# Hybrid decoder trunk on one core: delta rule scaled from both sides, norms from transposed rows, first loads reordered

## The chip, the cores and the metric

The kernel runs on one core of a Trainium2 chip. The metric is the device time of one execution in microseconds; the kernel before takes 1268.85 us, the median of three runs (1268.23 to 1269.07).

## The reference, cut to what matters

Two layers, each a half-step feed-forward block (SwiGLU), a mixing block with three head groups (gated delta rule, windowed attention, spatial gating), cross attention into 256 memory tokens, and a second feed-forward block; then a final norm. All in float32, 256 positions by 1024 channels. The change touches the delta rule of the mixing block and the loads.

```python
def l2_normalize(x):
    return x * lax.rsqrt(jnp.sum(x * x, axis=-1, keepdims=True) + NORM_EPS)

q = l2_normalize(q.reshape(B, S, DN_HEADS, DN_HEAD_DIM)) * (DN_HEAD_DIM ** -0.5)
k = l2_normalize(k.reshape(B, S, DN_HEADS, DN_HEAD_DIM))
...
    kb = k * beta[..., None]
    lower = jnp.where(tri_strict, jnp.einsum('bhncd,bhnsd->bhncs', kb, k) * decay, 0.0)
    eye = jnp.eye(C, dtype=q.dtype)
    t_inv = lax.linalg.triangular_solve(eye + lower, ..., lower=True, unit_diagonal=True)
    u = jnp.einsum('bhncs,bhnse->bhnce', t_inv, v * beta[..., None])
    w = jnp.einsum('bhncs,bhnsd->bhncd', t_inv, kb * jnp.exp(gc)[..., None])
```

## The kernel before, in words

Activations stand transposed, channels on the 128 partitions and the 256 positions in the free dimension. Every large product is made of float32 operands split in two: ACT casts a weight chunk to a high part (tiles wr to wh), DVE subtracts it for the low part (wl), and PE multiplies the parts as fp32r matmuls into banks pg. A product of a 512-column operand (both parts of the activations side by side) and one of 256 columns stand for one 128x128 weight block (`mm2`), or three of 256 columns (`mm3`). Weight chunks are 512 KB; SyncE's queue (SP) loads them in order into four buffers wr.

`Plan` records all operations, then `schedule` (lines 192 to 361) orders them: it simulates the engines with a table of costs, takes on each engine the ready operation of the highest rank (the longest way to the end plus a boost), and on PE subtracts `HOLD` from the rank of an operation whose kind (fp32r or plain fp32) is not that of the last one. `emit` writes the instructions out in this order, so all of them carry line 378. DMAs on SP keep the order in which the program names them.

The start (`trunk`, line 494 on): ACT's queue loads x in four pieces of two channel blocks each (tiles one, from xT), SP's queue loads the gains (sm) and the first four weight chunks. Twelve plain matmuls on zeros keep PE at work until data is there. The first two columns of the feed-forward block run as four banks at once over those four chunks (`two` in `ffn`): 64 matmuls, 16 for each chunk, with a fifth and sixth bank following.

The feed-forward block's second half goes through 11 pairs of chunks of `w_down` (one `wchunk` of 1 MB for 16 weight blocks). Ahead of the first of them `between` is called: in layer 0 it issues the loads of the attention tables (cb, 1248 KB), sm of layer 1 and the last gain, and in both layers those of the memory tokens (`mem_load`, four times 256 KB).

The delta rule (`mixing`, line 864 on): `conv` makes k, q and v (tiles q, channels on partitions, four heads each). `rnorm` squares them on ACT (256 columns) and sums over the channels with plain matmuls against ones, for each head and each half t of the positions (tiles t into ps). beta times the norm's factor (bk) is spread over rows by matmuls against the identity (pb), and the decay mask E is multiplied with it before the product of k with itself. The triangular matrix is inverted in a ladder of levels (blocks of 2 to 64, `LEVELS`), each level two groups of small plain matmuls for both halves t (tiles Mb, tc, uc, Q), with copies on ACT, subtractions and 32x32 transposes on DVE between them. Then come v, k transposed by PE (vb, kt), and the chain of the two chunks: u0, s1, r1, v1, o0, o1 (each a group of four matmuls into one bank ps, moved out by ACT or DVE). While ladder and chain wait for ACT and DVE, PE runs the projections of the other head groups and of the memory keys.

Of the kernel before, what the change touches and what calls it, by code (L numbers as in the profile page):

```python
# [11 lines left out]
F32R = mybir.dt.float32r  # L12
# [5 lines left out]
P = 128  # L18
D = 1024
T = 256  # L20
# [116 lines left out]
class Plan:  # L137
# [9 lines left out]
    BEGIN, RAMP, SLOW, WARM = 0.73, 4.5, 2.6, 7.5  # L147
    KEEP = ("pg", "ps", "wh", "wl", "t")
    HOLD = 2.0
# [42 lines left out]
    def schedule(self, fixed=None):  # L192
# [85 lines left out]
        while left:  # L278
# [43 lines left out]
            if o["method"] == "dma_start":  # L322
                dma_next += e == "DMA"
                feed = max(feed, t + self.FLIGHT) + lat * (self.SLOW if feed < self.RAMP else 1.0)
                lat = feed - t
# [168 lines left out]
def trunk(tc, xT, memT, w, w2, ca_d, cb_d, sm_d, fin_d, lb_d, out):  # L494
# [3 lines left out]
    with ExitStack() as ctx:  # L498
# [25 lines left out]
        hP = [one([2, T]) for i in range(4)]  # L524
        h = [hP[d // 2][:, d % 2, :] for d in range(KD)]
        ca = one([NCA])
# [4 lines left out]
        plan.boost = 1000.0  # L531
        SY.dma_start(sm[0], sm_d[0])
# [166 lines left out]
        class Norm:  # L699
# [4 lines left out]
            def add(self, d, first=False):  # L704
                if self.g is not None:
                    self.x.append(gained(h[d], self.g[:, d:d + 1], xslot(d), first and d % 2 == 0))
# [6 lines left out]
        def ffn(norm, nxt, start=False, between=None):  # L713
# [50 lines left out]
            side = between() if between else None  # L764
            wt = None
# [60 lines left out]
        def mem_load():  # L826
            raw = [S([2, T]) for _ in range(4)]
            for i in range(4):
                SY.dma_start(raw[i], memT[:, 2 * i:2 * i + 2, :])
            return [raw[k // 2][:, k % 2, :] for k in range(KD)]  # L830

        def mem_operands(l):
            m = mem_load()
            if not mem_st:
                mem_st.append(Stats())
                for k in range(KD):
                    mem_st[0].add(m[k])
            return [gained(m[k], sm[l][:, S_XM + k:S_XM + k + 1], S([2, T], F32R))
                    for k in range(KD)]
# [24 lines left out]
        def mixing(l, norm, nxt, xm):  # L864
# [92 lines left out]
            def rnorm(ts, s):  # L957
                v = tiny("qv" + s, [8])
# [8 lines left out]
                for t in range(2):  # L967
                    DVE.tensor_scalar(v[:, 4 * t:4 * t + 4],
                                      pp[t].rearrange("p (a b) -> p a b", a=8)[:, 0:4, 0], EPS, None,
                                      op0=ALU.add)  # L970
                y = tiny("qr" + s, [8])
                rsqrt(y, v, "qn" + s)
                return y

            kT = conv(1, pk0)
            rk = rnorm(kT, "k")
            bk = tiny("bk", [8])
            DVE.tensor_tensor(bk, beta, rk, op=ALU.mult)
            qT = conv(0)
            vT = conv(2)  # L980
# [475 lines left out]
```

## Time and profile before

| what | value |
|---|---|
| median of three runs | 1268.85 us (1268.23 to 1269.07) |
| the profiled execution's own time | 1268.92 us |
| its span, first to last instruction | 1267.1 us |
| mean granted TensorE clock | 0.997 |
| instructions in the span | 22194 |
| DMA, bytes and mean rate | 216.14 MB, 171 GB/s |

Times in the rows are microseconds from the span's start. A group of a timeline or a list of instructions names the engine, the operation, the tile written, the tiles read, the shape and how many instructions it merges. A plain fp32 matmul has two records in the trace, an fp32r matmul and a transpose have one. A matmul's recorded end is modelled; matmuls overlap, so the distance from one start to the next is what one costs in a sequence.

### The profile page before, as it was taken

The numbers are of one execution on the slowest core, as the hardware profiler recorded it, in microseconds if no ns is written. First come the engines' busy times: TensorE is split into PE (matmuls) and PEld (weight loads), VectorE is DVE, ScalarE is ACT, GpSimd is POOL, SyncE is SP. The second block draws the span as 40 slices with busy tenths as digits, with TensorE's granted clock in tenths as the row PEclk, the third lists the DMA queues.
The fourth block names the chain that finished last, engine by engine and source line by source line (L and its number), as shares of the span: only waits on it lengthen the run. The fifth ranks groups of instructions, "written<-read, shape, count | busy, mean of one in ns | idle before, by whom it ended". The sixth has DMA issues, their size and how long they took to land.

```text
span 1267.1 us, 22194 instructions
## 1 busy us (share of the span) xinstructions
PE 1249.3 (99%) x8400; PEld 1128.6 (89%) x8400; DVE 955.6 (75%) x1777; ACT 722.9 (57%) x1289; POOL 26.5 (2%) x69
## 2 busy tenths in 40 slices
PE   8999999999999999999999999999999999999997
PEld 7888889998898988888988888999899989888886
DVE  7776878987875777777677776799978667777764
ACT  6555755835654655555455565576466455655552
POOL 1000000100000000000000000001000000000000
PEclk9999999999999999999999999999999999999998
DMA  6555765433354455556555566554324544555551
GB/s 238 191 192 197 231 213 174 151 117 120 98 182 153 137 179 190 191 170 204 191 178 188 186 203 208 208 171 147 102 100 144 177 146 137 189 190 183 190 192 68
DMA packets 60730, 216.14 MB, mean 171 GB/s; under 512 B 7120, under 2 KB 7504, under 8 KB 60496
## 3 DMA queue, kind: packets, MB, share of 16 engines
q1 hardware_dynamic: 60048, 213.68, 50.8%
q8 instruction: 66, 1.08, 0.4%
q10 hardware_dynamic: 576, 1.05, 0.2%
q14 instruction: 40, 0.33, 0.1%
HBM read 213.65 MB, written 1.05 MB: 169 GB/s over the span
## 4 chain that ended last, share of the span: by engine, by line
PE 76%; issue 15%; DVE 4%; DMA 2%; ACT 2%; ACTq 0%; SPq 0%; POOLq 0%; POOL 0%; DVEq 0%
PE pg L378 69%; PE ps L378 7%; DVE S L378 2%; DVE wl L378 2%; ACT S L378 1%; ACT wh L378 1%; DMA wr<-w 1%; DMA one<-xT 1%; DMA one<-cb 0%; DMA S<-memT 0%; DVE t L378 0%; ACT L378 0%; ACTq L378 0%; DVE xmx L378 0%; ACT t L378 0%
## 5 line engine op out<-in xcount | busy, mean ns | idle before, releaser
L378 ACT CAST wh<-wr 128x1024 fp32r<-128x1024 f32 (+2 forms) x397 | 415.0, 1047 | 434.7 <-issue 245.5
L378 DVE TENSOR_TENSOR wl<-wr,wh 128x1024 fp32r<-128x1024 f32 (+2 forms) x397 | 484.7, 1222 | 229.4 <-ACT wh L378 228.3
L378 PE MATMUL pg<-X,wh 128*128 128x512 f32 (+1 forms) x2224 | 627.6, 353 | 2.1 <-ACT wh L378 2.1
L378 PE MATMUL pg<-X,wl 128*128 128x256 f32 x1808 | 478.5, 281 | 1.1 <-DVE wl L378 0.9
L378 PEld LDWEIGHTS pg<-X,wh 128*128 128x128 f32 x2224 | 378.3, 188 | 49.2 <-ACT wh L378 3.0
L378 PE MATMUL pg<-S,wh 128*128 128x256 f32 (+1 forms) x1560 | 385.2, 327 | 0.7 <-DVE S L378 0.7
L378 PEld LDWEIGHTS pg<-X,wl 128*128 128x128 f32 x1808 | 339.9, 188 | 18.1 <-DVE wl L378 3.7
L378 PE MATMUL pg<-S,wl 128*128 128x256 f32 x1088 | 300.9, 281 | 1.1 <-DVE wl L378 1.1
L378 PEld LDWEIGHTS pg<-S,wh 128*128 128x128 f32 x1560 | 259.3, 188 | 26.3 <-DVE S L378 1.1
L378 PEld LDWEIGHTS pg<-S,wl 128*128 128x128 f32 x1088 | 204.6, 188 | 3.7 <-DVE wl L378 1.4
L378 DVE TENSOR_TENSOR t<-t,pg 128x256 f32<-128x256 f32 x202 | 83.0, 414 | 2.2 <-ACT t L378 2.2
L378 ACT COPY t<-pg 128x256 f32<-128x256 f32 x202 | 73.0, 365 | 12.5 <-PE pg L378 12.5
L378 DVE TENSOR_TENSOR t<-t,t 128x256 f32<-128x256 f32 x157 | 66.0, 422 | 10.7 <-ACT t L378 3.2
L378 PE MATMUL ps<-S,S 128*128 128x256 f32 (+4 forms) x384 | 48.3, 291 | 2.7 <-ACT S L378 1.7
L378 DVE TENSOR_TENSOR t<-t,rbh 128x256 f32<-128x256 f32 x116 | 48.3, 420 | 1.3
L378 PEld LDWEIGHTS ps<-S,S 128*128 128x128 f32 (+2 forms) x384 | 42.0, 178 | 7.4 <-ACT S L378 3.5
L378 PE MATMUL pg<-wh,X 128*128 128x264 f32 (+2 forms) x192 | 45.0, 323 | 0.0
L378 ACT CAST S<-t 128x256 fp32r<-128x256 f32 x88 | 35.8, 407 | 10.2 <-DVE t L378 10.2
L378 ACT ACTIVATE t<-t 128x256 f32<-128x256 f32 x88 | 36.5, 420 | 7.8 <-DVE t L378 7.7
L378 PE MATMUL pg<-wh,S 128*128 128x512 f32 x128 | 40.8, 395 | 0.0
L378 DVE TENSOR_TENSOR S<-t,S 128x256 fp32r<-128x256 f32 x88 | 36.9, 419 | 2.0 <-ACT S L378 1.9
L378 ACT ACTIVATE t<-one 128x256 f32<-128x256 f32 x72 | 29.5, 412 | 8.6 <-DVE one L378 7.7
(184 smaller groups left out, 865.7 us busy)
## 6 DMA issues: line engine op xcount, KB each, us to landing
wr<-w SPq DMA_DIRECT2D x391, 512.0 KB, 3.3
wr<-w SPq DMA_DIRECT2D x4, 528.0 KB, 3.3
S<-memT SPq DMA_DIRECT2D x8, 256.0 KB, 5.9
lb<-lb SPq DMA_DIRECT2D x2, 640.0 KB, 4.6
one<-cb SPq DMA_DIRECT2D x1, 1248.0 KB, 6.1
one<-xT ACTq DMA_DIRECT2D x4, 256.0 KB, 5.5
out<-S SPq DMA_DIRECT2D x3, 256.0 KB, 2.2
wr<-w SPq DMA_DIRECT2D x2, 256.0 KB, 5.3
```

Source lines behind the costliest of these rows:

```text
L378: getattr(self.engines[o["eng"]], o["method"])(*[real(a) for a in o["args"]], **{k: real(a) for k, a in o["kw"].items()})
```

## The change

In the delta rule `rnorm` transposes the four heads of k (and of q) with PE into a bank, and ACT squares each head's 128 columns straight from the bank with a running sum (`accum_out`), which gives the sum of squares with positions on partitions; the eight matmuls against ones go. The transposed first half of k is kept (kt0), so that the later transposition of k goes. The triangular system is scaled on both sides: the spreading of bk over rows (eight matmuls pb) goes, the mask is multiplied with bk of the row, v is multiplied with kn (factor times sum of squares) in place of beta, and u0 and v1 are multiplied with bk as they leave the bank, on DVE in place of an ACT copy. The planner's `HOLD` goes from 2.0 to 3.0, and its costs of early loads change.

The loads: the first piece of x gets the gains of the first norm behind it (x0), ACT's queue loads x0, half of the first weight chunk and the second chunk, SP's queue all else in the order of use, sm last. The memory pieces, and in layer 0 after them the attention tables in four pieces, sm and the last gain, are issued one behind each chunk pair of the second half of the feed-forward block.

```diff
-    BEGIN, RAMP, SLOW, WARM = 0.73, 4.5, 2.6, 7.5
+    BEGIN, RAMP, SLOW, WARM = 0.73, 10.0, 1.33, 7.5
-    HOLD = 2.0
+    HOLD = 3.0
...
-        SY.dma_start(sm[0], sm_d[0])
-        for i in range(4):
-            SA.dma_start(hP[i], xT[i])
-            for c in ((slice(0, 512), slice(512, 1024)) if i == 0 else (slice(0, 1024),)):
-                SY.dma_start(first[i][:, c], w[i][:, c])
+        SA.dma_start(x0, x0_d)
+        SY.dma_start(first[0][:, lo], w[0][:, lo])
+        SA.dma_start(first[0][:, hi], w[0][:, hi])
+        SY.dma_start(hP[1], xT[0])
+        SA.dma_start(first[1][:, 0:1024], w[1])
+        SY.dma_start(hP[2], xT[1])
+        SY.dma_start(first[2][:, 0:1024], w[2])
+        SY.dma_start(hP[3], xT[2])
+        SY.dma_start(first[3][:, 0:1024], w[3])
+        SY.dma_start(sm[0], sm_d[0])
...
         def late_consts():
-            SY.dma_start(cb, cb_d)
-            SY.dma_start(sm[1], sm_d[1])
-            SY.dma_start(fin, fin_d)
+            c = [slice(i * NCB // 4, (i + 1) * NCB // 4) for i in range(4)]
+            return [lambda s=s: SY.dma_start(cb[:, s], cb_d[:, s]) for s in c] + [
+                lambda: SY.dma_start(sm[1], sm_d[1]), lambda: SY.dma_start(fin, fin_d)]
...
                     if i % 16 == 0:
                         wt = wchunk()
+                        if later:
+                            later.pop(0)()
...
-                pp = [sbank([256]) for _ in range(2)]
-                for i in range(NH):
-                    sq = tmp()
-                    act(sq, ts[i], AF.Square)
-                    for t in range(2):
-                        PE.matmul(pp[t][:, 32 * i:32 * i + P], lhsT=sq[:, t * P:t * P + P],
-                                  rhs=ones, start=True, stop=True)
+                for t in range(2):
+                    ps = hmm(lambda o, i: PE.transpose(o, ts[i][:, tsl(t)], ident))
+                    for i in range(NH):
+                        act(tmp(P), ps[:, i, :], AF.Square, accum_out=v[:, 4 * t + i:4 * t + i + 1])
+                    rows.append(ps)
...
+            rk, vk, krows = rnorm(kT, "k")
+            kt0 = S([NH, P])
+            ACT.copy(kt0, krows[0])
...
-                pb = hmm(lambda o, i: PE.matmul(
-                    o, lhsT=bk[:, 4 * t + i:4 * t + i + 1].to_broadcast([P, P]), rhs=ident,
-                    start=True, stop=True))
                 eb = S([NH, P])
-                DVE.tensor_tensor(eb, es, pb, op=ALU.mult)
+                DVE.tensor_tensor(eb, es, bcl(bk[:, 4 * t:4 * t + 4]), op=ALU.mult)
...
-                DVE.tensor_tensor(v, ps, bcl(beta[:, 4 * t:4 * t + 4]), op=ALU.mult)
+                DVE.tensor_tensor(v, ps, bcl(kn[:, 4 * t:4 * t + 4]), op=ALU.mult)
...
-            ps = hmm(lambda o, i: PE.transpose(o, kT[i][:, 0:P], ident))
-            kt = S([NH, P])
-            DVE.tensor_tensor(kt, ps, bcl(kc), op=ALU.mult)
+            kt = kt0
+            DVE.tensor_tensor(kt, kt, bcl(kc), op=ALU.mult)
...
-            ACT.copy(u0, ps)
+            DVE.tensor_tensor(u0, ps, bcl(bk[:, 0:4]), op=ALU.mult)
...
-            ACT.copy(v1, ps)
+            DVE.tensor_tensor(v1, ps, bcl(bk[:, 4:8]), op=ALU.mult)
```

How the order of the instructions moves, at three places. First the start, on SP's queue and on ACT's: before, SP issues the gains, then the weight chunks (wr from w; the first chunk in two halves).

```order
L378 DMA one_6_69<-sm 128x97
L378 DMA wr_83<-w 128x512 x2
L378 DMA wr_100<-w 128x1024
L378 DMA wr_106<-w 128x1024
L378 DMA wr_112<-w 128x1024
L378 DMA one_5_119<-ca 128x256
```

With the change, the same stretch of SP's queue (xT are three of the four pieces of x), and ACT's queue up to its first cast of a weight chunk:

```order
L378 DMA wr_69<-w 128x512
L378 DMA one_2_82<-xT 128x512
L378 DMA one_3_92<-xT 128x512
L378 DMA wr_98<-w 128x1024
L378 DMA one_4_104<-xT 128x512
L378 DMA wr_110<-w 128x1024
L378 DMA one_6_117<-sm 128x97
L378 DMA one_5_126<-ca 128x256
```

```order
L378 DMA one_1_63<-x 128x520
L378 DMA wr_69<-w 128x512
L378 DMA wr_90<-w 128x1024
L378 ACT_TABLE_LOAD
L378 ACTIVATE X_120<-one_1_63 128x256
L378 ACTIVATE t_130<-one_1_63 128x256
L378 ACTIVATE t_132<-one_1_63 128x256
L378 CAST wh_136<-wr_69 128x512 x2
```

Three of the four x pieces moved from ACT's queue to SP's, half of the first weight chunk and all of the second the other way; the gains moved behind all of these.

Second, SP's queue in layer 0 at the second half of the first feed-forward block, before (cb are the attention tables, memT the memory tokens):

```order
L378 DMA wr_1356<-w 128x1024
L378 DMA one_15_1360<-cb 128x2496
L378 DMA one_7_1365<-sm 128x97
L378 DMA one_8_1372<-fin 128x8
L378 DMA S_1378<-memT 128x512
L378 DMA S_1386<-memT 128x512
L378 DMA S_1393<-memT 128x512
L378 DMA S_1399<-memT 128x512
L378 DMA wr_1404<-w 128x1024
```

and with the change, where the pattern goes on with three more memT and then the four pieces of cb:

```order
L378 DMA wr_1365<-w 128x1024
L378 DMA wr_1406<-w 128x1024
L378 DMA S_1413<-memT 128x512
L378 DMA wr_1438<-w 128x1024
L378 DMA wr_1471<-w 128x1024
L378 DMA S_1480<-memT 128x512
```

Seven loads in one block became one load behind every two weight chunks.

Third, PE in the ladder of layer 0, its first two groups of small matmuls and what stands between them (tc and Mb into one bank for each half t, then Q and uc), before:

```order
L378 MATMUL ps_3202<-tc_85,Mb_3130 64x64 x4
L378 MATMUL ps_3209<-tc_89,Mb_3136 64x64 x4
L378 MATMUL pg_3195<-X_1775,wh_3052 128x256 x2
L378 MATMUL pg_3195<-X_1775,wl_3061 128x256
L378 MATMUL pg_3195<-X_1854,wh_3052 128x256 x2
L378 MATMUL pg_3195<-X_1854,wl_3061 128x256
L378 MATMUL pg_3195<-X_1933,wh_3052 128x256
L378 MATMUL ps_3234<-Q_96,uc_3112 64x64 x4
L378 MATMUL ps_3239<-Q_104,uc_3118 64x64 x4
```

and with the change:

```order
L378 MATMUL ps_3315<-tc_84,Mb_3196 64x64 x4
L378 MATMUL ps_3324<-tc_96,Mb_3210 64x64 x4
L378 MATMUL ps_3329<-one_5_126,q_2749 128x128
L378 MATMUL pg_3260<-wh_3262,X_1995 128x512
L378 MATMUL pg_3260<-wl_3273,X_1995 128x512
L378 MATMUL pg_3260<-wh_3262,X_1995 128x512
L378 MATMUL pg_3260<-wh_3262,X_2074 128x512
L378 MATMUL ps_3347<-Q_88,uc_3187 64x64 x4
L378 MATMUL ps_3352<-Q_102,uc_3204 64x64 x4
```

The ladder now starts later in PE's order, beside the projection with 512 columns, and a single transposition of v (ps from q) stands behind each group.

## Rows read from the trace of the kernel before

**Rows 1.** Page, section 1: busy us, share of the span, instructions of PE.

```profile
PE 1249.3 (99%) x8400; PEld 1128.6 (89%) x8400; DVE 955.6 (75%) x1777; ACT 722.9 (57%) x1289; POOL 26.5 (2%) x69
```

**Rows 2.** PE's waits: released by which engine's tile, us in total, times, longest.

```profile
PE ps L378 <- ACT S L378: 1.7, 2, 0.9
...
PE ps L378 <- DVE S L378: 0.9, 2, 0.5
```

**Rows 3.** Groups by form, PE: shapes, count, busy us, mean ns, idle before.

```profile
L378 PE MATMUL ps<-one,q 128*128 128x128 f32 x24 | 4.3, 286 | 0.0
...
L378 PE MATMUL ps<-one,bk 128*128 128x128 f32 x32 | 3.9, 275 | 0.0
```

**Rows 4.** Timeline, PE, mixing of layer 0: start, us, operation [idle before].

```profile
257.18 1.95 PE L378 MATMUL ps<-one,bk 128*128 128x128 f32 x16
258.96 1.06 PE L378 MATMUL ps<-q 128*128 128x128 f32 x8
...
297.25 0.66 PE L378 MATMUL ps<-one,q 128*128 128x128 f32 x4
297.66 0.48 PE L378 MATMUL pg<-S,wh 128*128 128x256 f32 x2
```

**Rows 5.** Timeline, PE, the start.

```profile
1.05 5.49 PE L378 MATMUL ps<-one 128*128 128x128 f32 x24 [1.05 <-DVE one L378]
6.94 0.73 PE L378 MATMUL pg<-X,wh 128*128 128x512 f32 x2 [0.40 <-ACT wh L378]
...
14.21 0.40 PE L378 MATMUL pg<-X,wh 128*128 128x512 f32 x1
14.44 0.28 PE L378 MATMUL pg<-X,wl 128*128 128x256 f32 x1
14.56 0.40 PE L378 MATMUL pg<-X,wh 128*128 128x512 f32 x1
...
21.64 0.39 PE L378 MATMUL ps<-X,wh 128*128 128x512 f32 x1
```

**Rows 6.** Windows: stretch, its us, busy us by engine, clock, DMA share, GB/s.

```profile
0.00:5.00 5.00, 3.95 (x18) 3.95 (x19) 1.00 (x3) 2.36 (x4) 2.95 (x21) 1.00 0.62 188
```

**Rows 7.** DMA queues from 3 to 6 us, q1 SP's, q10 ACT's: packets, MB, share.

```profile
q1 hardware_dynamic: 275, 0.51, 64.2%
q10 hardware_dynamic: 296, 0.53, 47.9%
```

**Rows 8.** Timeline, ACT and DVE, the start.

```profile
11.29 1.03 ACT L378 CAST wh<-wr 128x1024 fp32r<-128x1024 f32 x1
11.30 0.42 DVE L378 TENSOR_TENSOR t<-t,t 128x256 f32<-128x256 f32 x1
11.63 0.48 DVE L378 SCALAR_TENSOR_TENSOR X<-one,one,X 128x256 fp32r<-128x256 f32 x1
...
12.35 1.23 DVE L378 TENSOR_TENSOR wl<-wr,wh 128x1024 fp32r<-128x1024 f32 x1 [0.23 <-ACT wh L378]
```

**Rows 9.** Timeline, SP, PE and ACT, second half of the feed-forward block, both layers.

```profile
120.26 0.43 SPq L378 DMA_DIRECT2D one<-cb  x1
...
132.89 0.39 PE L378 MATMUL pg<-X,wl 128*128 128x256 f32 x1 [0.67 <-DVE wl L378]
...
135.00 1.05 ACT L378 CAST wh<-wr 128x1024 fp32r<-128x1024 f32 x1 [1.32 <-DMA wr<-w]
...
140.02 0.39 PE L378 MATMUL pg<-S,wl 128*128 128x256 f32 x1 [1.13 <-DVE wl L378]
...
756.43 0.39 PE L378 MATMUL pg<-X,wl 128*128 128x256 f32 x1 [0.28 <-DVE wl L378]
```

**Rows 10.** Timeline, PE, two steps of the ladder in layer 0.

```profile
269.56 1.15 PE L378 MATMUL ps<-tc,Mb 128*64 128x64 f32 x16
...
271.65 1.15 PE L378 MATMUL ps<-Q,uc 128*64 128x64 f32 x16
```

**Rows 11.** Windows: the ladder of layer 0 (PE, PEld, DVE, ACT, POOL).

```profile
269.56:309.88 40.32, 40.32 (x363) 35.03 (x362) 34.17 (x88) 20.76 (x44) 1.59 (x8) 1.00 0.36 118
```

More of the change, by code (lines that the diff above doesn't have):

```diff
@@ L323, in schedule @@
                 dma_next += e == "DMA"
-                feed = max(feed, t + self.FLIGHT) + lat * (self.SLOW if feed < self.RAMP else 1.0)
+                feed = max(feed, t + self.FLIGHT + 0.3 * (t < 1.0)) + lat * (self.SLOW if feed < self.RAMP else 1.0)
                 lat = feed - t
@@ L521, in act @@
             ACT.activation(o, i, f, **kw)
-        hP = [one([2, T]) for i in range(4)]
+        x0 = one([2 * T + KD])
+        hP = [x0[:, 0:2 * T].rearrange("p (a b) -> p a b", a=2)] + [one([2, T]) for i in range(3)]
         h = [hP[d // 2][:, d % 2, :] for d in range(KD)]
+        gain0 = x0[:, 2 * T:]
         ca = one([NCA])
@@ L705, in add @@
                 if self.g is not None:
-                    self.x.append(gained(h[d], self.g[:, d:d + 1], xslot(d), first and d % 2 == 0))
+                    self.x.append(gained(h[d], self.g[:, d:d + 1], xslot(d), first and d == 0))
                 else:
@@ L763, in ffn @@
             plan.boost = 0.0
-            side = between() if between else None
-            wt = None
+            wt, side, later = None, None, []
+            if between:
+                side, later = between()
             for d in range(KD):
@@ L824, in trunk, with mem_operands, two @@
         mem_r, mem_st = [], []
[L826 to L833, printed above, removed]
+        def mem_operands(l, xm):
             if not mem_st:
                 mem_st.append(Stats())
[L836 to L839, printed above, removed]
+            def two(i):
+                raw = S([2, T])
+                SY.dma_start(raw, memT[i])
+                for e in range(2):
+                    k = 2 * i + e
+                    if l == 0:
+                        mem_st[0].add(raw[:, e, :], boost=0.0)
+                    xm.append(gained(raw[:, e, :], sm[l][:, S_XM + k:S_XM + k + 1], S([2, T], F32R)))
+            return [lambda i=i: two(i) for i in range(4)]
         def mem_keys(xm):
@@ L955, in conv @@
                 return res
-            def rnorm(ts, s):
-                v = tiny("qv" + s, [8])
-                pp = [sbank([256]) for _ in range(2)]
-                for i in range(NH):
-                    sq = tmp()
-                    act(sq, ts[i], AF.Square)
-                    for t in range(2):
-                        PE.matmul(pp[t][:, 32 * i:32 * i + P], lhsT=sq[:, t * P:t * P + P],
-                                  rhs=ones, start=True, stop=True)
[L967 to L980, printed above, removed]
-            rq = rnorm(qT, "q")
             def tsl(t):
@@ L990, in hmm, with rnorm @@
                 return ps
+            def rnorm(ts, s):
+                v = tiny("qv" + s, [8])
+                rows = []
+                for t in range(2):
[3 more added lines that the diff above has]
+                    rows.append(ps)
+                DVE.tensor_scalar(v, v, EPS, None, op0=ALU.add)
+                y = tiny("qr" + s, [8])
+                rsqrt(y, v, "qn" + s)
+                return y, v, rows
+            kT = conv(1, pk0)
+            rk, vk, krows = rnorm(kT, "k")
+            kt0 = S([NH, P])
+            ACT.copy(kt0, krows[0])
+            bk = tiny("bk", [8])
+            DVE.tensor_tensor(bk, beta, rk, op=ALU.mult)
+            kn = tiny("kn", [8])
+            DVE.tensor_tensor(kn, rk, vk, op=ALU.mult)
+            qT = conv(0)
+            vT = conv(2)
+            rq = rnorm(qT, "q")[0]
             M, A, U, Mc, Uc, Tc, Qc = [], [], [], [], [], [], []
@@ L1110, in mixing @@
             r1 = S([NH, P])
-            DVE.tensor_tensor(r1, ps, bcl(wc), op=ALU.mult)
+            DVE.tensor_tensor(r1, ps, bcl(egs[:, 0:4]), op=ALU.mult)
             DVE.tensor_tensor(r1, vb[1], r1, op=ALU.subtract)
@@ L1312, in cross @@
             proj_add(ops, range(KD), nxt)
-        norm = Norm(sm[0][:, S_F1:S_F1 + 8])
+        norm = Norm(gain0)
         for d in range(KD):
@@ L1321, in side @@
             def side():
-                if l == 0:
-                    late_consts()
-                return mem_operands(l)
+                xm = []
+                return xm, mem_operands(l, xm) + (late_consts() if l == 0 else [])
             xm = ffn(norm, nxt, l == 0, side)
@@ L1348, in _pack @@
     ins = {}
-    ins["xT"] = f["x"][0].reshape(T, KD // 2, 2, P).transpose(1, 3, 2, 0)
-    ins["memT"] = f["mem"][0].reshape(T, KD, P).transpose(2, 1, 0)
+    t = f["x"][0].reshape(T, KD // 2, 2, P).transpose(1, 3, 2, 0)
+    ins["x0"] = np.concatenate([t[0].reshape(P, 2 * T), f["ffn1_norm"][0].reshape(KD, P).T], 1)
+    ins["xT"] = t[1:]
+    ins["memT"] = f["mem"][0].reshape(T, KD // 2, 2, P).transpose(1, 3, 2, 0)
     def cols2(wm, c0, c1):
```

10 lines of the change are left out of this document (6 added, 4 removed).

## The prediction

> **What bounds the kernel now.** I read the page's busy times first, then what PE waited for, then PE's timeline where the change works. PE is busy in 99% of the span [rows 1], so the question for each part is what it takes from PE's sequence or from PE's few waits. The waits that the profile names are small; those for bank contents in the delta rule (on ACT S and DVE S) come to 2.6 us in the whole span [rows 2]. The recorded length of a matmul is no price, since matmuls overlap: the spread of bk has 0.275 us for each record [rows 3], but eight of these matmuls, 16 records, start at 257.18 and the next group at 258.96 [rows 4], which is 0.2225 us for a matmul. The starts are the prices below.
>
> **The change part by part.**
>
> *Norms and scaling of the delta rule.* For each layer 16 plain matmuls against ones (k and q, four heads, two halves) and eight for the spread of bk go: 24 x 0.2225 = 5.34 us. Sixteen transposes for the norms come and four for k go, so 12 more. Four transposes start at 297.25 and the next work at 297.66 [rows 4]: 0.10 us each, 1.23 us for 12. Net 4.1 us for a layer, **8.2 us** for two, all of it on PE's own sequence.
>
> Here a row and a rule stand apart. The transposes' recorded mean is 0.286 us [rows 3], their distance 0.10. The Trainium skill (TensorE: Matmul & The Clock Gate, Part 4: PE-mode transpose) gives about 275 ns for a 128x128 transpose within a kernel, which agrees with the recorded length; taken as the price it would leave 4.1 us of this term. I take the distance, since it is what PE's sequence shows; the other is a rival below.
>
> What moves to other engines: for each norm eight ACT squares of 128 columns with a sum in place of four of 256, for u0 and v1 a DVE product in place of an ACT copy, and an ACT copy for kt0. In the order of the changed program two whole projections (96 matmuls of 256 columns, 96 x 0.12 = 11.5 us) stand between the transposes of k and the first product that needs its norm, so I cost them at nothing; without that cover the squares alone would be some microseconds a layer. In the chain behind the ladder, a DVE product replaces an ACT copy of the same 512 elements twice; PE's waits there could shrink by some of the 2.6 us [rows 2], or grow. I take zero between a gain of 1.3 (half of them) and a loss that the first rival prices.
>
> *Kept together longer (`HOLD`).* I counted how often PE goes over from fp32r to plain fp32 work: 73 times before, 72 with the change. Into groups of 64-column products, the ladder's among them, it goes 24 times in each program. So no term; what it does is to change what stands between the ladder's steps.
>
> *The start.* Warm-up products run to 6.54, the first real one starts at 6.94, and the next bank's work begins at 21.64 [rows 5]. Between lie 64 products over four chunks, 32 of 512 columns at 0.23 (14.21 to 14.44) and 32 of 256 at 0.12 (14.44 to 14.56) [rows 5]: 11.2 us, 2.8 a chunk. So 3.9 us of the stretch is something else: two sums for the norm, which stay (I take 0.4, two plain matmuls), and waits for data, 3.5. That is the upper bound of the gain. For the lower bound, nothing: the same bytes come through the same engines.
>
> My value follows the second chunk, now third on ACT's queue. Both queues got about the same bytes while both had work: 0.51 and 0.53 MB in three microseconds, 0.35 MB/us together [rows 7]. ACT's three loads are 1.05 MB, so with as much from SP's queue 2.1 MB have moved when this chunk is there; 0.94 MB have by 5.0 (188 GB/s) [rows 6], the rest takes 3.3, so 8.3. The cast takes 1.03 (the ACT row at 11.29) [rows 8]: 9.4, and PE, through with the first chunk at 6.54 + 2.8 = 9.34, waits 0.1. The low part takes 1.23 [rows 8], to 10.65, four products of high parts 0.93, so 0.25 more. From then on DVE sets the pace: two operands at 0.48, two additions at 0.42 and one low part at 1.23 [rows 8] make 3.03 for a chunk against PE's 2.8, and in the fourth chunk the low part is wanted with the second product already; carried through, that is 0.3 and 0.5 us. Waits 1.15, and 0.1 for each of four restarts: 1.55 against 3.5, so **2.0 us** less. The gains' load goes to the end of SP's queue, but they come with x0, and sm is first needed long after. What is late next is therefore DVE's low part, not a load.
>
> *The loads inside the feed-forward block.* In layer 0 the attention tables are issued in one piece at 120.26, with the memory tokens behind; ACT then waits 1.32 us at 135.00 for a weight chunk, and PE twice for a low part, 0.67 at 132.89 and 1.13 at 140.02. Layer 1, with the memory tokens alone, has 0.28 at 756.43 [rows 9]. With the change a load of 0.26 to 0.32 MB follows every 1.05 MB of weights; 1.37 MB take 3.9 us at 0.35 MB/us [rows 7], and PE needs 16 x 0.35 = 5.6 for the blocks of such a chunk [rows 5]. So all of these waits should go: **2.1 us**, bounds 0 and 2.1. What comes with the memory pieces (squares, gained parts on ACT and DVE) is the same work, spread over four chunks.
>
> *Sum.* 8.2 + 2.0 + 2.1 = 12.3 us from the profiled execution's 1268.92, which is 0.07 over the median: **1256.6 us**. The end of the kernel is not touched.
>
> **The rivals.**
>
> *The ladder and chain become exposed.* PE's removed work stood beside a chain through ACT and DVE that isn't shorter. If that chain sets the end of the mixing block, PE waits for what it no longer does. At worst all 8.2 us come back: 1264.8. For it: the chain already has most of PE's named waits in this block [rows 2]. Against: in the ladder PE was busy in all of 40.32 us [rows 11], so PE and not the chain set its pace, and its tightest steps, 269.56 to 271.65, 2.09 us [rows 10], held with no idle time. In the changed order the same step has a transpose and four products of 512 columns between its groups, 0.10 + 0.93 us, in place of seven of 256, 0.83; no later step is given less than the tightest of before, but for the last group of the ladder.
>
> *The loads bring nothing.* Start and tables move the same bytes, and the two queues share the engines; were the data as late as before, only the PE term is left: 1260.7. For it: the first 13 us run near the measured rate. Against: the order of need brings the first 0.77 MB together, and the waits at 132.89 and 140.02 stand beside one block of loads.
>
> *A transpose costs its recorded length.* 24 more transposes at 0.286 in place of 0.10 cost 4.4 us: 1261.0. The starts in [rows 4] speak against it. The Trainium skill's 275 ns (same page and section) would come to nearly this.
>
> *Slower: the ladder is late by one big operation at each step.* Two layers, five levels of two steps: 20 steps, each a short ACT copy or DVE subtraction that PE waits for. In order behind a low part (1.23 us [rows 8]) each would come that much later: 24.6 us, so 1256.6 + 24.6 = 1281.2. It decides from about 0.75 us a step, where the 12.3 us are gone and 2.5 more. For it: DVE was busy for 34.17 of the ladder's 40.32 us [rows 11], and u0 and v1 now need it too. Against: the same share left PE no idle time before.
>
> That the change doesn't take the work from PE is ruled out: the built program has 24 matmuls fewer, 48 plain ones out and 24 transposes in.
>
> **How the numbers follow.** Forecast 0.70; the exposed ladder and chain 0.11; loads without effect 0.12; dear transposes 0.04; the late ladder 0.03. A measurement of this kernel can tell some 0.2% (2.5 us) from no change. All cases but the last are faster by more, except where the first rival also meets a start that gains nothing: faster 0.93, same 0.04, slower 0.03. The range goes down to all upper bounds nearly together (8.2 + 3.5 + 2.1 + 1.3 = 15.1, so 1253.8; I write 1253.5) and up past the loads rival and the dear transposes, and through the better part of the first rival: 1262.5.
>
> **What would show it.** Right: PE's plain 128-column products against ones in the delta rule and the spread of bk gone; the first real product right behind the warm-up, and the fifth bank's first product near 19.6 in place of 21.64; no PE wait for a low part near 130 to 140; PE still near 99% busy, the mixing block of a layer about 4 us shorter. Wrong: new PE waits for S, Mb, Q or uc in the ladder or chain (the first or the last rival), waits for wh in the first 20 us (the loads), or groups of four transposes more than 0.15 us apart.

## The result, and the profile after

The changed kernel takes 1255.55 us (1254.98 to 1255.83, four runs), the kernel before 1268.54 on the same chip (1268.01 to 1269.07, four runs): a ratio of 0.9897 (95% interval 0.9881 to 0.9913), 13.0 us less. 12.3 less had been forecast. The profiled execution has a span of 1254.1 us where before it was 1267.1.

PE's busy time fell with the span, DVE's is the same to the tenth (955.6 us), and ACT has 1.4 us more; the rows of before are [rows 1]. The page of the changed kernel, section 1:

```profile
PE 1238.5 (99%) x8328; PEld 1119.5 (89%) x8328; DVE 955.6 (76%) x1774; ACT 724.3 (58%) x1338; POOL 28.2 (2%) x69
```

So PE is still what sets the time; its busy time fell by 10.8 us, the idle time beside it makes the rest. The list of PE's waits after the change (who released it, us in total, times, longest), against [rows 2]:

```profile
PE ps L378 <- DVE S L378: 1.8, 3, 0.7
PE ps L378 <- ACT S L378: 1.6, 2, 0.8
...
PE ps L378 <- DVE rcm L378: 1.3, 1, 1.3
...
PE pg L378 <- DVE wl L378: 0.2, 1, 0.2
```

The same list of before has 2.1 us for high parts (wh) and this for low parts (wl):

```profile
PE pg L378 <- DVE wl L378: 2.1, 3, 1.1
```

So the waits for weight parts are down to 0.2 us, the waits for S on ACT and DVE have grown by 0.8 us in all, and one is new in this list: 1.3 us for rcm, the factor of the memory tokens' norm.

Where the time went is best read from the starts of PE's matmuls, cut at the same product of both programs (in us; the forecast beside it):

| stretch | before | after | change | forecast |
|---|---|---|---|---|
| start, to the fifth bank | 21.87 | 19.51 | -2.36 | -2.0 |
| layer 0, first half of the feed-forward block | 78.23 | 77.81 | -0.42 | 0 |
| its second half, to 165 us | 65.00 | 64.27 | -0.73 | -1.8 |
| on to the mixing block | 34.59 | 34.60 | 0 | 0 |
| mixing, layer 0 | 167.99 | 164.13 | -3.86 | -4.1 |
| cross and second feed-forward block, layer 0 | 270.04 | 269.68 | -0.36 | 0 |
| first feed-forward block, layer 1 | 183.31 | 182.72 | -0.59 | -0.3 |
| mixing, layer 1 | 168.12 | 164.68 | -3.44 | -4.1 |
| from there to the last matmul | 271.43 | 270.46 | -0.97 | 0 |

The three parts of the change show, and besides them 1.75 us in three stretches that it doesn't touch. Of the last one's 0.97 us, 0.26 belong to the execution and not to the program. The granted clock of PE fell near the end, after idle times of 1.43 and 1.61 us. In the profile of before it is 0.50 (the level of 1.2 GHz) from 1259.5 us on, and the last four records start 0.37 and then 0.21 us apart; in that of the changed kernel it is still 1.00 (2.4 GHz) there, and they start 0.21 and then 0.11 apart:

```profile
1259.98 1.22 PE L378 MATMUL ps<-one,rch 128*128 128x128 f32 x4 [1.61 <-DVE rch L378]
```

```profile
1247.53 0.71 PE L378 MATMUL ps<-one,rch 128*128 128x128 f32 x4 [1.61 <-DVE rch L378]
```

The changed kernel's second profile (after_again, below) has the clock at 0.50 there and 1.22 us again. That profile also bounds what a single stretch can tell: its start is 0.33 us longer and its stretch from 97 to 161 us (the third line) 0.35 shorter than in the first.

**The start.** PE's timeline after the change (start, us, operation, idle before), against [rows 5]:

```profile
6.37 0.50 PE L378 MATMUL pg<-X,wh 128*128 128x512 f32 x1
7.10 0.39 PE L378 MATMUL pg<-X,wl 128*128 128x256 f32 x1 [0.23 <-DVE wl L378]
...
9.85 1.19 PE L378 MATMUL pg<-X,wh 128*128 128x512 f32 x4
11.11 0.74 PE L378 MATMUL pg<-X,wl 128*128 128x256 f32 x4
...
13.08 1.09 PE L378 MATMUL pg<-X,wh 128*128 128x512 f32 x4
14.00 0.65 PE L378 MATMUL pg<-X,wl 128*128 128x256 f32 x4
...
15.87 0.40 PE L378 MATMUL pg<-X,wh 128*128 128x512 f32 x1
...
19.28 0.39 PE L378 MATMUL ps<-X,wh 128*128 128x512 f32 x1
```

The first real product stands right behind the warm-up here, but that is chance: in after_again the warm-up ends at 5.40, since its products go from 0.21 to 0.11 us apart sooner, and the first product starts at 6.70, after 1.29 us of waiting for ACT's high part. The chunks begin at 6.37, 9.85, 13.08 and 15.87; the third takes 2.79 us, which is PE's own pace, the first two 3.48 and 3.23, the fourth 3.41 with 0.37 for the norm's sums. The fifth bank's first product is at 21.05 to 21.64 in the three profiles with the old loads and at 18.90 to 19.61 in the ten with the new ones, so the 2.36 us are good to some 0.5; between the means lie 2.1. The second chunk was there for ACT at 8.75 (8.3 had been forecast):

```profile
8.75 1.05 ACT L378 CAST wh<-wr 128x1024 fp32r<-128x1024 f32 x1 [0.48 <-DMA wr<-w]
```

**The mixing block.** PE's timeline of layer 0 after the change; ps<-one,q are transposes (in groups those for the norms, single ones those of v), ps<-one,g and ps<-q plain matmuls, and 64-column products are the ladder's:

```profile
250.78 0.27 PE L378 MATMUL ps<-one,q 128*128 128x128 f32 x1
250.89 1.06 PE L378 MATMUL ps<-one,g 128*128 128x128 f32 x8
251.78 1.06 PE L378 MATMUL ps<-q 128*128 128x128 f32 x8
252.68 0.93 PE L378 MATMUL ps<-one,q 128*128 128x128 f32 x7
253.36 0.36 PE L378 MATMUL pg<-wh,X 128*128 128x256 f32 x1
...
273.37 1.15 PE L378 MATMUL ps<-tc,Mb 128*64 128x64 f32 x16
274.44 0.33 PE L378 MATMUL ps<-one,q 128*128 128x128 f32 x1
274.53 0.47 PE L378 MATMUL pg<-wh,X 128*128 128x512 f32 x1
...
275.62 1.15 PE L378 MATMUL ps<-Q,uc 128*64 128x64 f32 x16
```

Seven transposes start at 252.68 and the next product at 253.36: 0.10 us each. The groups by form (shapes, count, busy us, mean ns, idle before) have the transposes with a recorded mean of 0.293 us, and no group ps<-one,bk any more, against [rows 3]:

```profile
L378 PE MATMUL ps<-one,q 128*128 128x128 f32 x48 | 10.1, 293 | 0.0
```

The ladder's first two steps (273.37, 275.62) are 2.25 us apart, 2.09 in [rows 10], with no idle time ahead of them, and the window over the ladder, up to the first product of the chain behind it (304.95), has PE busy in every microsecond, as [rows 11] had:

```profile
273.37:305.00 31.63, 31.63 (x313) 27.80 (x312) 28.87 (x80) 15.42 (x37) 1.59 (x8) 1.00 0.33 104
```

Outside of this window PE waits more than before: 0.65 us at 314.67 (0.47 at 319.98 before), and in layer 1 one wait is new, ahead of the product of k with itself:

```profile
871.12 0.94 PE L378 MATMUL ps<-q,q 128*128 128x128 f32 x6 [0.53 <-DVE S L378]
```

**The loads.** The waits at 132.89, 140.02 and 756.43 [rows 9] are gone. In their place the timeline of all engines has this, from DVE's low part to the product that spreads rcm over the partitions:

```profile
148.62 1.22 DVE L378 TENSOR_TENSOR wl<-wr,wh 128x1024 fp32r<-128x1024 f32 x1
...
149.75 0.15 DVE L378 TENSOR_SCALAR rv<-ps 128x2 f32<-128x2 f32 x1
...
149.98 0.70 POOL L378 TENSOR_TENSOR rcm<-rv,one 128x2 f32<-128x2 f32 x1 [130.95 <-DVE rv L378]
...
151.32 0.16 DVE L378 SCALAR_TENSOR_TENSOR rcm<-rna,rcm 128x2 f32<-128x2 f32 x1
...
151.53 0.71 PE L378 MATMUL ps<-one,rcm 128*128 128x128 f32 x4 [1.31 <-DVE rcm L378]
```

Five short operations on DVE and POOL, one behind the other, with a low part ahead of the first: the factor leaves DVE 0.05 us before PE's product starts. In the kernel before the spreading product started 3.6 us after its factor was done. By the trace, what makes the factor late begins at ACT, which waits for the last memory piece:

```profile
144.19 0.73 ACT L378 ACTIVATE t<-S 128x256 f32<-128x256 f32 x2 [2.15 <-DMA S<-memT]
```

Behind these squares stands the cast of a weight chunk (145.62), behind that DVE's low part (146.68), the one at 148.62 and then the factor's first operation at 149.75; in in_one, where ACT doesn't wait for memory tokens at this place, it is at 148.34.

### The profile page after: what moved, and what is told of

The parts are those of the page before. It is cut to its first block, busy times and chain, and to the rows that moved or that the text cites. A ratio compares the mean times of both kernels' runs of the same rounds, so it can differ in the third digit from the quotient of the medians.

```text
span 1254.1 us, 22081 instructions
## 1 busy us (share of the span) xinstructions
PE 1238.5 (99%) x8328; PEld 1119.5 (89%) x8328; DVE 955.6 (76%) x1774; ACT 724.3 (58%) x1338; POOL 28.2 (2%) x69
## 3 DMA queue, kind: packets, MB, share of 16 engines
q10 hardware_dynamic: 432, 1.05, 0.2%
HBM read 213.66 MB, written 1.05 MB: 171 GB/s over the span
## 4 chain that ended last, share of the span: by engine, by line
PE 79%; issue 15%; DVE 3%; ACT 1%; DMA 1%; POOL 0%; ACTq 0%; POOLq 0%; DVEq 0%
PE pg L378 72%; PE ps L378 7%; DVE S L378 2%; DVE wl L378 1%; ACT wh L378 1%; DMA wr<-w 1%; ACT S L378 0%; POOL qrk L378 0%; DVE mx L378 0%; ACT L378 0%; POOL brs L378 0%; DVE xmx L378 0%; ACTq L378 0%; DVE q L378 0%; POOLq L1463 0%
```

## The experiments

All times are medians beside the kernel before on the same chip and in the same rounds: 1267.46 us for the first four, 1268.29 for the next four, 1268.08 for the last four. A ratio stands with its 95% interval.

### dr_only: the delta rule's part alone

The edit to the kernel before: norms from transposes and scaling from both sides, as in the change's hunks in `rnorm` and `mixing`; loads, `HOLD` and the planner's costs stay.

> The kernel before with the delta rule's part of the change alone (norms from transposed rows, scaling from both sides); loads, HOLD and the planner's load costs as before. Theory (the gain is PE's own sequence: 48 plain matmuls out at 0.2225 us, 24 transposes in at 0.10): about 8.2 us less than before, 1260.3 or within 1 us of it. Rival (the ladder and the chain set the end of the mixing block): 4 us less or fewer, with new PE waits for Mb, Q, uc or S. Rival (a transpose costs its recorded 0.286 us): 3.8 us less.

Measured: 1261.94 us (1260.21 to 1262.34), ratio 0.9950 (0.9936 to 0.9963). Both mixing blocks are shorter by what they are in the full change: 3.82 and 3.33 us (3.86 and 3.44). But the total gains only 5.5 us, less than the theory's 7.2 to 9.2. Part of it is given back in layer 1's feed-forward block, which this edit doesn't touch: its second half takes 85.70 us in place of 84.84, with the same order of products, since PE waits 0.9 us for low parts there in place of 0.3 (PE's waits from 730 to 825 us; the first line is of this kernel, the second of the kernel before):

```profile
PE pg L378 <- DVE wl L378: 0.9, 2, 0.6
```

```profile
PE pg L378 <- DVE wl L378: 0.3, 1, 0.3
```

Why isn't shown. That the mixing block ends sooner is not needed for it: in placed (below), whose blocks end as late as before, the wait there is 0.57 us. With the change's loads it is gone.

### loads_only: start and loads alone

The edit to the kernel before: the start's loads, gains with x0, memory tokens (laid out as in the changed kernel) and tables spread over the chunks, and the planner's load costs; the delta rule and `HOLD` stay.

> The kernel before with the loads alone (x0 and the order at the start, memory and tables spread behind weight chunks, the planner's load costs); delta rule and HOLD as before. Theory: 2.0 to 2.4 us at the start and 1 to 2 us in the feed-forward block, together 3 to 4.1 us less than before. Rival (the same bytes are as late as before): no difference over 0.5 us.

Measured: 1264.22 us (1262.75 to 1265.41), ratio 0.9973 (0.9963 to 0.9984). The start is 2.5 us shorter, but the stretch from 100 to 165 us takes 65.08 against 65.00: nothing gained. The list of PE's waits of this kernel says why:

```profile
PE ps L378 <- DVE t L378: 2.0, 1, 2.0
...
PE pg L378 <- DVE wl L378: 0.2, 1, 0.2
```

The waits for low parts are gone here as well, and 2.0 us go to t, the memory tokens' squares, whose sum PE wants before the last pieces have come and been squared. It is the same norm that makes the 1.3 us for rcm in the full change.

### hold2: the changed kernel with `HOLD` at its old value

```diff
-    HOLD = 3.0
+    HOLD = 2.0
```

> The changed kernel with HOLD back at 2.0. In the built order PE goes over from fp32r to plain fp32 work 75 times in place of 72. Theory of the prediction (no term for HOLD): within 0.5 us of the changed kernel. Rival (each such group costs some 0.3 us around its edges): about 0.9 us slower than the changed kernel.

Measured: 1256.31 us (1256.11 to 1256.49), ratio 0.9908 (0.9895 to 0.9922), span 1254.3 us against 1254.1. `HOLD` is worth nothing that can be told apart from zero; the rival's 0.9 us lie within the interval too, and only the spans, 0.2 us apart, speak against it.

This run shows one thing more. The two parts alone brought 5.5 and 3.2 us; together, in this kernel and in the same rounds, it is 11.2, so 2.4 more than their sum. The profiles show 1.3 of it, 0.8 of this in layer 1's feed-forward block, where dr_only's added wait is gone; the rest isn't placed.

### t_twice: the transposes for the norms issued twice

```diff
                     ps = hmm(lambda o, i: PE.transpose(o, ts[i][:, tsl(t)], ident))
+                    for i in range(NH):
+                        PE.transpose(ps[:, i, :], ts[i][:, tsl(t)], ident)
```

> The changed kernel with the 32 transposes of the two norms (both layers) issued twice into the same banks. Theory (0.10 us for a transpose in a sequence): 3.3 us slower than the changed kernel. Rival (a transpose costs its recorded 0.286 us): 9.2 us slower.

Measured: 1262.55 us (1261.57 to 1264.41), ratio 0.9959 (0.9947 to 0.9972), 6.2 us more than hold2 beside it. The two mixing blocks take 6.3 us more than in the changed kernel, 0.2 for each of 32 transposes: between the two prices. PE's timeline of this kernel shows that it is two things:

```profile
253.16 1.04 PE L378 MATMUL ps<-one,q 128*128 128x128 f32 x8
254.04 1.95 PE L378 MATMUL ps<-q 128*128 128x128 f32 x16
...
277.68 0.68 PE L378 MATMUL ps<-tc,Mb 128*64 128x64 f32 x8
278.29 0.33 PE L378 MATMUL ps<-one,q 128*128 128x128 f32 x1
278.37 0.48 PE L378 MATMUL pg<-wl,X 128*128 128x512 f32 x1
278.78 0.68 PE L378 MATMUL ps<-Q,uc 128*64 128x64 f32 x8
```

Eight transposes in 0.88 us are 0.11 each, so 32 cost 3.5. The rest, 2.8 us, is the planner's answer: it cut steps of the ladder in two (8 records in place of 16), and half a step takes 0.61 us (277.68 to 278.29) where a whole one takes 1.07 (273.37 to 274.44 above), so 0.15 for each of three cuts in a layer. Two more changes from fp32r to plain work in each layer, and in layer 1 a wait of 0.68 us for tc that the changed kernel doesn't have, are in it as well. So the price of a transpose is the distance, 0.11 us. The Trainium skill (TensorE: Matmul & The Clock Gate, Part 4: PE-mode transpose) gives about 275 ns; the recorded length agrees with it (0.293 in the changed kernel), the time that a transpose takes from PE's sequence does not.

### after_again: the changed kernel, unedited

> The changed kernel once more, without an edit, as the mark for the three others on this chip. Expected: the ratio of the first comparison, 0.990 of the kernel before (0.988 to 0.992), some 1255 us; a ratio outside of 0.987 to 0.993 would mean that the chip, not the program, sets a part of the difference.

Measured: 1256.09 us (1255.80 to 1256.48), ratio 0.9904 (0.9891 to 0.9918). It is the mark for the next three.

### m_late: the memory norm's factor without a boost

```diff
-                plan.boost = 60.0
+                plan.boost = 60.0 if tag == "h" else 0.0
```

> The changed kernel, but the factor of the memory tokens' norm is placed without a boost, so its spread over the partitions comes later in PE's order. Theory: the 1.31 us that PE waits at 151.53 for rcm is a matter of order alone (the factor is put into PE's order before VectorE can have it) and goes: the stretch from 100 to 165 us shrinks by 1.1 to 1.4, the whole by about 1.3 us against the changed kernel. Rival: the factor is late because VectorE is, and whatever needs VectorE's next low part waits then instead: less than 0.3 us.

Measured: 1257.75 us (1256.84 to 1257.86), ratio 0.9916 (0.9902 to 0.9929): slower by 1.7 us. Neither theory. The stretch from 100 to 165 us did lose 2.2 us against the mark (61.73 in place of 63.92, in part since four small products left it), but the wait came back in the mixing block, longer:

```profile
240.41 0.68 PE L378 MATMUL ps<-one,rcm 128*128 128x128 f32 x4 [1.61 <-DVE rcm L378]
```

and with these products there the planner gave layer 0 the same cut-up ladder as in the run with doubled transposes: 168.0 us for the block in place of 164.1. In this run too the factor's spread stands in PE's order ahead of when it can be done, though its rank is lower.

### placed: the kernel before, its tiles where the changed kernel has them

```diff
+        for tag in """one1s0 one9s0 one11s0 wrs0 xss0 xss1 ... fnas1""".split():
+            sb.tile([P, 1], F32, tag=tag, name="place_" + tag)
         for o in order:
...
-        hP = [one([2, T]) for i in range(4)]
+        x0 = one([2 * T + KD])
+        hP = [x0[:, 0:2 * T].rearrange("p (a b) -> p a b", a=2)] + [one([2, T]) for i in range(3)]
```

> The kernel before with its order untouched, but every tile in SBUF at the address that it has in the changed kernel (the tiles' tags are named in that kernel's order ahead of the first instruction, and the first input tile is 8 columns wider). Theory: 256-column products start 0.1170 us apart in the changed kernel and 0.1179 before because of where the operands lie; then the feed-forward and cross blocks take the changed kernel's times (the feed-forward block behind the first cross block 0.3 to 0.5 us less, the one of layer 1 0.4 each half, about 1.5 to 2.0 us in all), with nothing gained at the start, in the mixing blocks' groups or in the waits at 130 to 140. Rival: the pace comes from the other order of the loads; then the time is that of the kernel before, within 0.4 us.

Measured: 1268.17 us (1267.49 to 1270.12), ratio 1.0002 (0.9993 to 1.0010): no change. The theory falls as it was put: the addresses of the tiles' slots alone do not bring the shorter untouched blocks (the second feed-forward block of layer 0 takes 186.19 us, 186.02 before, 185.72 after). More on this in the last section.

### in_one: memory tokens and tables in one piece again

```diff
                 side, later = between()
+                while later:
+                    later.pop(0)()
...
-                return xm, mem_operands(l, xm) + (late_consts() if l == 0 else [])
+                return xm, (late_consts() if l == 0 else []) + mem_operands(l, xm)
```

> The changed kernel, but the memory tokens and tables are loaded in one piece where the down projection begins, tables first, as before. Theory: the waits for low parts behind that block of loads (0.67, 1.13 and 0.28 us in the kernel before) come back, and the 1.31 us wait for the memory norm's factor changes with the earlier squares: between 0.5 and 2.1 us longer than the changed kernel. Rival: spreading the loads brings nothing by itself, since what is saved at the low parts is given back at the factor: within 0.4 us of the changed kernel, or shorter.

Measured: 1254.12 us (1253.48 to 1254.34), ratio 0.9887 (0.9872 to 0.9902): 2.0 us under the mark, and the ranges of the two don't touch. The theory was wrong in its sign. The stretch from 100 to 165 us takes 62.93 (63.92 in the mark). Windows over it (us, busy us of PE, PEld, DVE, ACT, POOL, clock, DMA share, GB/s), of the changed kernel first:

```profile
100.00:165.00 65.00, 63.69 (x366) 55.46 (x365) 50.04 (x90) 38.68 (x72) 0.70 (x1) 1.00 0.67 215
```

```profile
100.00:165.00 65.00, 65.00 (x373) 56.50 (x372) 50.18 (x90) 41.21 (x76) 0.70 (x1) 1.00 0.68 220
```

With the loads in one block PE is idle for nothing, 1.31 us with the loads spread. The waits for low parts did not come back, and the one for rcm went. So spreading the loads isn't needed to remove the old waits, and it is what made the new one.

### in_one_again: the same once more

> The version with the memory tokens and tables loaded in one piece, tables first and in four parts, once more as the mark for the next two. Expected: the ratio of its first run, 0.9887 of the kernel before (0.9872 to 0.9902), about 2 us under the changed kernel.

Measured: 1253.60 us (1253.21 to 1253.72), ratio 0.9885 (0.9869 to 0.9901). It holds, and it is the mark for the next two.

### mem_first: memory tokens together, tables spread

```diff
-                return xm, mem_operands(l, xm) + (late_consts() if l == 0 else [])
+                for f in mem_operands(l, xm):
+                    f()
+                return xm, late_consts() if l == 0 else []
```

> The changed kernel, but the four loads of the memory tokens are issued together where the down projection begins, and only the tables are spread over the weight chunks behind. Theory: what the spreading of the change cost is the lateness of the memory tokens, whose norm's factor PE then waits for (1.31 us at 151.53); with them early that wait is gone, and the spread tables cost nothing: the stretch from 100 to 165 us takes 62.9 within 0.4, the whole within 0.5 us of the version in one piece. Rival: every load between two weight chunks delays a low part, however it is ordered: waits for wl of some tenths each, 1 us or more longer than the version in one piece.

Measured: 1255.23 us (1254.85 to 1255.35), ratio 0.9898 (0.9884 to 0.9912). The wait for rcm is gone and the stretch from 100 to 165 us takes 62.98, as the theory had it; so it is the late memory tokens that cost. But the total is 1.6 us above the version in one piece, of which only 0.5 lie in the first 165 us: the rest is spread over blocks whose PE order is the same in both.

### cb_one: in one piece, and the table undivided

```diff
-            c = [slice(i * NCB // 4, (i + 1) * NCB // 4) for i in range(4)]
+            c = [slice(0, NCB)]
```

> The version in one piece, but the tables are one load of 1.25 MB again in place of four of 0.31. Theory: dividing the table is what took the waits for low parts away, since the one load took 6 us to land and held the weights behind it; then waits for wl of 0.5 to 1.1 us come back near 130 and 138, and the stretch from 100 to 165 us is 1.2 to 2.0 longer than in the version in one piece. Rival: the size of the piece doesn't matter, and the waits were gone because PE reads the operands in another phase since the start is shorter: within 0.4 us.

Measured: 1253.81 us (1253.74 to 1254.22), ratio 0.9888 (0.9874 to 0.9902): the same as divided; the stretch takes 62.70 in both. The theory falls again. What then took the old waits away? The loads of this kernel are those of the kernel before in number, size and order. Its DMA issues from 116 to 126 us (count, size, median us to landing):

```profile
one<-cb SPq DMA_DIRECT2D x1, 1248.0 KB, 6.4
S<-memT SPq DMA_DIRECT2D x4, 256.0 KB, 5.9
```

and those of the kernel before:

```profile
one<-cb SPq DMA_DIRECT2D x1, 1248.0 KB, 6.1
...
S<-memT SPq DMA_DIRECT2D x4, 256.0 KB, 7.1
```

The table takes as long; the memory tokens land sooner. From the landing of the small gain (fin) ahead of them to that of the weight chunk behind them it is 3.8 us here, 3.8 and 3.7 in the two runs in one piece, and 5.3, 5.3 and 5.7 in the kernel before, in placed and in dr_only. What these loads differ in is their source: a piece of memT was cut out of rows that are four times as long, and is now a block of its own in memory. The description of the change doesn't name this. How late memory tokens reach PE can be read from ACT in the kernel before:

```profile
128.13 0.72 ACT L378 ACTIVATE t<-S 128x256 f32<-128x256 f32 x2 [0.87 <-DMA S<-memT]
...
129.88 1.05 ACT L378 CAST wh<-wr 128x1024 fp32r<-128x1024 f32 x1
```

The weight chunk of this cast had landed at 123.09. It waited for ACT, whose order has the squares of memory tokens ahead of it, and its low part is the one that PE waits for at 132.89. The second wait, at 140.02, has two parts: its chunk came late (134.93, the 1.32 us of ACT in [rows 9]), and DVE had seven other operations ahead of the low part. In this run ACT waits 0.23 us for memory tokens where it waited 0.87. The six profiles agree, but no run changed the layout alone: all three profiles with the old waits also have the old start, and ACT's and DVE's orders there are others. The layout is the likeliest cause, not shown.

### start_old: the first loads in their old order

```diff
-        SA.dma_start(x0, x0_d)
-        SY.dma_start(first[0][:, lo], w[0][:, lo])
-        SA.dma_start(first[0][:, hi], w[0][:, hi])
...
+        SY.dma_start(sm[0], sm_d[0])
+        SA.dma_start(x0, x0_d)
+        SY.dma_start(first[0][:, lo], w[0][:, lo])
+        SY.dma_start(first[0][:, hi], w[0][:, hi])
+        for i in range(1, 4):
+            SA.dma_start(hP[i], xT[i - 1])
+            SY.dma_start(first[i][:, 0:1024], w[i])
```

> The changed kernel with the start's loads in the order and on the queues of the kernel before (the gains still come with the first input tile). Theory: the start's gain is lost and nothing else; the fifth bank's first product goes back from 19.28 to 21.3 to 21.7, and all of it reaches the end: 2.0 to 2.4 us longer than the changed kernel. Rival: the time is given back behind the start, where low parts or loads are waited for sooner: less than 1 us.

Measured: 1258.55 us (1257.79 to 1261.57), ratio 0.9929 (0.9915 to 0.9943), by the ratios 3.2 us more than the changed kernel (after_again), which is over the theory's 2.0 to 2.4. PE's timeline of its start:

```profile
5.99 0.74 PE L378 MATMUL pg<-X,wh 128*128 128x512 f32 x2
8.90 0.96 PE L378 MATMUL pg<-X,wh 128*128 128x512 f32 x3 [0.97 <-ACT wh L378]
...
11.88 1.20 PE L378 MATMUL pg<-X,wh 128*128 128x512 f32 x4 [1.28 <-ACT wh L378]
...
13.28 0.38 PE L378 MATMUL pg<-X,wl 128*128 128x256 f32 x1 [0.21 <-DVE wl L378]
...
21.88 0.40 PE L378 MATMUL ps<-X,wh 128*128 128x512 f32 x1
```

PE starts sooner here and still gets to the fifth bank 2.6 us later: 2.25 us are two waits for the second and third chunk. The start's gain is the chunks' place in the queues, and it reaches the end.

## Why the prediction was right, and where it was not

*Norms and scaling: forecast 8.2, measured 7.3 us (3.86 and 3.44), right.* From the starts of PE's matmuls in the two blocks, each up to the next start: the 48 plain matmuls against ones and for bk took 10.8 us (5.35 and 5.46), 10.7 in the sum; the 24 added transposes cost 2.45 (1.22 and 1.23), 0.10 each, as in the sum. So the two prices hold. What the sum lacks is 1.1 us by which the other products of the blocks are longer: PE's waits for S grew by 0.8 us, 0.53 of it at the new wait of layer 1, which by the starts costs 0.7. The prediction took these waits as zero, between a gain of 1.3 and the first rival's loss. That rival's exposed ladder did not come (no idle time from 273.37 to 305.00); waits beside the ladder did, 0.8 us of the 8.2 that were at stake. The rival with the recorded length, 0.286, is out by t_twice.

*`HOLD`: no term, and none seen* (hold2, whose interval can't tell 0.9 us from nothing).

*The start: forecast 2.0, measured 2.4 (2.1 between the means of all profiles), right.* Load order was the cause (start_old). What was late next was DVE's low part, as the prediction put it, but in the first two chunks, not in the third and fourth: 0.23 us of named wait at 7.10, which the sum lacked, and 0.34 at 11.11 (11.11 less 9.85 and four products of 0.23), against 0.25. With those two behind it DVE had caught up, and the 0.3 and 0.5 us that were carried through to later chunks weren't seen.

*The loads inside the feed-forward block: forecast 2.1, measured 1.3 (0.73 in layer 0, 0.54 for the wait in layer 1), too large, and for a wrong reason.* The waits went, as forecast; but the step "with the change a load of 0.26 to 0.32 MB follows every 1.05 MB of weights", from which it followed, isn't why: they stay away with all loads in one block (in_one, cb_one). The reading behind it was off as well. ACT's wait for a weight chunk at 135.00 comes after PE's first wait at 132.89; that one was for memory tokens in ACT's order, not for weights. And the sentence that what comes with the memory pieces "is the same work, spread over four chunks" left out who waits for that work: ACT, whose casts of weights stand behind it, and PE at the norm's factor. That is a rival that should have been written down: a wait that takes the place of the one removed. The price was wrong too. By the starts, with the slower product behind each wait, the three waits cost 0.93, 1.26 and 0.54 us, 2.7 together, where their named idle times make 2.1; so 2.1 was no upper bound. The new wait costs 1.57 where 1.31 is named. In layer 0 that makes 0.93 + 1.26 - 1.57 = 0.62 of the 0.73 measured.

*What no step had.* Stretches that the change doesn't touch are 1.75 us shorter (0.42, 0.36, 0.97 in the table), and from the last cut to the end of the span it is 0.24 more; 0.26 of the first and a part of the second come with the clock at the end. Two terms were too large by 0.9 and 0.8 us, the start too small by 0.4, and these 2 us lifted the sum again: 12.3 forecast, 13.0 measured. That the sum is close is partly luck.

## What to carry to other kernels

Where PE is busy all the time, price a removed or added matmul by the distance of starts within its group, not by its recorded length, and add what a short group costs at its ends; price a wait by the starts too (0.54 us for a named 0.28 here). When a load is spread out to clear the way for others, follow the spread data to all its consumers and look at what stands behind them in each engine's order, and where the last one stands in the order of the engine that sets the time; here undoing the spread and keeping everything else gave the fastest kernel, 1253.6 us, 2.0 below the changed one by in_one. A planner that orders everything answers a local edit in other places (85.70 for 84.84 us in dr_only, the cut-up ladder in t_twice and m_late), so an edit's worth has to be read by stretch, and then once more in the total.

## What was not expected of the hardware

The same fp32r products in the same order take a different time in different programs, and the same time again and again in one. 474 products of the last feed-forward block's first half take 83.01 and 83.03 us in the kernel before and dr_only, 83.14 in placed, 82.76 in mem_first and cb_one, and 82.56 or 82.57 in the other nine profiles. No wait is named there. Between the two profiles of the changed kernel no product's distance differs by 0.005 us, nor between the kernel before and dr_only, or cb_one and mem_first. Between the kernel before and the changed one some 65 do, at the same place of each group: 0.235 us to the next start before and 0.225 after, for instance, twenty times in this stretch. Placed has the order of the kernel before and only other addresses in SBUF, and there some 150 distances changed, by as much, in both directions. So the place of the data is the likeliest cause, worth some 0.010 us for a product and up to 0.6 for a block of 83 us; the traces hold no addresses, so it isn't shown product by product. The slots' addresses alone don't bring the changed kernel's times (placed), and what rule does is open. It is the likeliest source of most of the time that no step of the prediction had.
